# Low parts by VectorE instead of adding transfers, two fresh banks at the end and later gate rows in a diffusion transformer step

## The chip, the cores and the metric

One core of one Trainium2 chip runs the whole step. The metric is the device time of one execution in microseconds (us). TensorE (PE) multiplies; VectorE (DVE), ScalarE (ACT) and GpSimd (POOL) work on tiles; SyncE (SP) and POOL issue the transfers (DMA) that this text speaks of.

## The reference

One layer for 128 prompt tokens and 128 sample tokens, width 2048, all in float32. Both attention mixers use the result of one projection.

```python
sh1, sc1, g1, sh2, sc2, g2 = ada_mod(c, w_ada, b_ada)
h = rms_norm(x, norm1_w) * (1 + sc1) + sh1
qa, ka, va, qb, kb, vb, ga, gb = project_heads(h, w_in, ...)
oa = window_attention(qa, ka, va, ...)
ob = neighbourhood_attention(qb, kb, vb, ...)
x = x + g1 * ((sigmoid(ga) * (oa @ w_br_a) + sigmoid(gb) * (ob @ w_br_b)) @ w_out)
h2 = rms_norm(x, norm2_w) * (1 + sc2) + sh2
x = x + g2 * (square(relu(h2 @ w_up)) @ w_down)      # w_up 2048 x 8192, w_down 8192 x 2048
```

## The kernel before

Each weight tile of 128 x 1024 float32 numbers (512 KB) is a *step*; 456 steps, numbered 0 to 455, are multiplied in a fixed order. The matmuls take operands of the type fp32r (the profile names it), and every operand is split into a high part (`wH`, a copy by ScalarE at L108) and a low part (`wL`, the raw tile minus the high part, by VectorE at L268). A product is three matmuls: high by high, low by high, high by low. A plain step has twelve matmuls of 512 columns: three for each half of the tile and each of the two streams of tokens (prompt and sample).

The steps are: 0 to 72 the projection, 73 to 135 its gate columns, 136 to 199 the merge, 200 to 215 the first up columns. Then seven *pairs* follow, p = 1 to 7: sixteen steps of the up projection (`up_pair`, from step 216 + 32(p − 1)) and sixteen of the down projection (`down_unit`, four units of four steps). The last sixteen steps are the down projection of the last columns, where each unit ends in `resid`: VectorE multiplies the sum by the gate rows (`t<-g,acc`, L1138) and adds the residual (`x1b<-x1b,t`, L1142), and SyncE stores the result. The last unit (`last_unit`, steps 452 to 455) ends its second stream of tokens in two halves of 256 columns, so that the store of the first half can start.

In an up stage some of the eight positions are *fast* (list `FAST`): two weight tiles x and y give seven products in place of eight, of which the operands are made from the tiles. A fast position has these, with their lines: ScalarE's copies XH, YB (first half), tH, uH, and on VectorE t = x + y (L1465), XL (L1469), two sums in place (`raw`, L1470 and L1473), the low half of YB (L1472), tL (L1475) and uL (L1476). XL and YB's low half can also be made without VectorE: `minus_plus` lets ScalarE write minus the high part (L274), and a transfer issued by POOL then adds the weights from memory to it (L275). The lists `XL_DMA` and `YL_DMA` name the positions (8p + position) where this is done, and `LO_DMA` the plain steps. A value above zero is the number of steps by which the transfer goes ahead of its use; zero leaves it where the position is prepared.

The order on every engine is the order of the program, and that is made by `run()`: before the matmuls of a step it issues loads up to RUN further steps, then the adding transfers that are due, prepares the steps up to LOOK further (high and low parts), and copies high parts of AHEAD steps more. LOOK, RUN and AHEAD are strings with one digit for each step. Tiles come from a ring of 50 buffers of 512 KB; a load waits until its buffer has been read for the last time. The partial sums of the down projection (`dsum`) are put back as start values (*seeds*, `acc<-dsum`, by ScalarE) into the banks at the next pair's down units, and `DS_AWAY` names those that wait in memory meanwhile. `TE` names the heads whose probabilities TensorE transposes (L963); the others go through a transposing transfer. Gate columns of the projection that wait in memory (`AWAY`) come back GATE_BACK steps ahead, and the modulation of the layer is made beside the projection from `araw` tiles.

Of the kernel before, what the change touches and what calls it, by code (L numbers as in the profile page):

```python
# [18 lines left out]
P = 128  # L19
# [16 lines left out]
H_AT = 42  # L36
DOTS1 = [19, 26, 29, 33, 34, 34, 40, 42]
# [11 lines left out]
ADA_LD = [1, 0, 0, 2, 1, 0, 0]  # L49
BEGIN_SEED = ()  # L50
FAST = {1: (0, 1, 3, 7), 2: (0, 2, 4, 7), 3: (0, 3, 4, 5, 7), 4: (0, 2, 4, 6, 7), 5: (0, 1, 3, 6, 7), 6: (0, 1, 3, 6, 7), 7: (0, 2, 3, 5, 7)}
AWAY = [('gB', 2), ('gB', 0), ('gA', 0)]
GATE_BACK = 7
SEED_IN = {3: 0, 4: 1}
SEED_AT = 4
DIRECT = (3,)
LO_DMA = {123: 3, 162: 4, 196: 6, 205: 8, 233: 5, 421: 5, 452: 5}

LOOK = "220102342600004321112333333423344346003343323264425550024766435445100474621316521154444204744421242145443452135211233544444376555544342442445533113321545566643343457745545676631233475557402456897561133345442776554653214434322546645533234767635734543210333332754523544642203425555547355455542235444454346622143243143533120323340312252123324443413423323622444434555345666437402100223322544523544524557200014130212545432212544243022242111444300005772000137786"
RUN = "143538999224623021111226444342023133100001316655554435733333554564563325525103544635357136486300020025420321354421003432333255533612243352667454523663311454555543535997565577799967554203545745166866764795556988745674676472100044367288985999944454243112133555665422126411011224421346635244575533444454353423332446683456501300223410454545542322431521552123100123853233511252576696622311441202144625734434231022445134778334434464132124568676567978669999987788"  # L60
AHEAD = "822111111111101110000000111111110000000000122222221000000000000011122211000020133110000100000233100000000000002200000000000001112000000000000111000000100000000000000000011100000011111232221244332110000000000000000000000003011311110000000002000000000001020000000000000000000000000000002220001100100000000000000000000000000100000000000000001000222222222322320000000000000000000010000000000100000000000000000000000000000211110000000100000000012444242132345400"
CONST_AT = [63, 75]
XL_DMA = {9: 0, 11: 11, 16: 0, 20: 8, 23: 6, 26: 0, 29: 0, 36: 0, 37: 0, 38: 0, 43: 0, 46: 5, 53: 0, 54: 0, 63: 0}
ADA_G = ((1,), (2,), (3, 4), (5, 6))
ADA_AT = [None, 5, 14, 20, 22, 37, 38]
XS_AT = {1: 9, 2: 24, 3: 37}
POST = {('kvA', 0): [66, 70, 73], ('qA', 0): [65, 71, 75, 75, 77], ('qA', 1): [70, 74, 75, 76, 82], ('kB', 0): [74, 77, 79, 83, 85], ('qB', 0): [81, 82, 86, 88, 90], ('kB', 1): [84, 88, 91, 92, 97], ('qB', 1): [89, 92, 99, 100, 101]}
JOBS = [[79, 80, 82, 83, 85, 86, 89], [81, 83, 84, 86, 87, 92, 99], [86, 86, 87, 89, 91, 91, 106], [91, 92, 93, 96, 99, 105, 111], [93, 97, 99, 101, 101, 104, 115], [96, 101, 102, 104, 106, 106, 115], [106, 106, 108, 110, 117, 118, 125], [109, 111, 116, 117, 119, 123, 125]]
SS_G = [(0, 2), (2, 1)]
SS_AT = [50, 53, 71, 73, 131, 141]  # L70
T_AT = [3, 4]
PREP_IN = [6, 8]
DOTS = [33, 43, 47, 49, 50, 51, 52, 54, 56, 56, 56, 56, 60, 62, 63, 67, 70, 73, 80, 84, 89, 91, 92, 93, 96, 98, 102, 103, 104, 106, 108, 109, 109, 112, 114, 117, 118, 120, 122, 122, 126, 126, 129, 129, 129, 131, 132, 137, 138, 138, 140, 144, 145, 146, 154, 155, 156, 160, 160, 163, 167, 169, 173, 173, 175, 175, 179, 179, 180, 182, 184, 190]
DOTS2 = [222, 233, 234, 234, 235, 238, 245, 247, 254, 265, 269, 270, 272, 288, 300, 301, 304, 327, 328, 331, 333, 336, 349, 359, 360, 362, 364, 368, 393, 393, 395, 401]
STAT_AT = [4, -1, 9, 3]
T_PAIR = [[12, 6], [6, 10], [5, 10], [6, 10], [6, 10], [6, 10], [7, 12]]
P_PAIR = [[3, -1], [2, 4], [3, 3], [1, 4], [2, 5], [1, 5], [2, 0]]
M_TE = (3,)
M_AT = [2, 2, 5]
FLIP = 1  # L80
P_UP = [3, 3]
T_UP = [16, 11]
# [4 lines left out]
def tile_hybrid_step(ctx: ExitStack, tc: tile.TileContext, a):  # L87
# [143 lines left out]
    def add_step(src, mm, key, half=0, xkey=None):  # L231
# [10 lines left out]
        lead = LO_DMA.get(st["i"], 0) or XL_DMA.get(xkey, 0)  # L242
        load_at(st["i"] - LOAD - max(0, lead - LOAD), load)
# [64 lines left out]
    by_dma, xl_steps = [], []  # L308

    def run():  # L310
        loads.sort(key=lambda x: x[:2])
# [1496 lines left out]
```

## Time and profile before

| | us |
|---|---|
| median of 3 runs (1321.24 to 1321.27) | 1321.27 |
| the profiled execution | 1321.1 |
| span of its trace | 1319.3 |
| TensorE busy | 1306.7 |
| VectorE busy | 1123.5 |
| ScalarE busy | 905.1 |
| POOL busy | 57.1 |

Matmuls are pipelined: each 512-column matmul is recorded as about 0.39 us long but the next begins 0.23 us after it. So a gap on TensorE is read from the starts. A bracket behind a row names how long the engine was idle before it and what ended that.

### The profile page before, as it was taken

What the parts mean: (1) busy time and instruction counts of PE and PEld (TensorE: products, weight loads), DVE (VectorE), ACT (ScalarE), POOL (GpSimd) and SP (SyncE); (2) the same over time, 40 slices, a digit from 0 to 9 for tenths busy, and PEclk for the clock granted to TensorE, in tenths of its full rate; (3) what the DMA queues carried; (4) which work ended last, traced back from release to release, by engine and by line L of the source; (5) the groups of instructions that cost most, each with busy time, mean ns of one, the idle gap of its engine ahead of it and who ended that gap; (6) DMA issues with size and microseconds to landing.
All of it is one profiled execution on the core that took longest, in us unless ns stands there. A gap on an engine that the chain in (4) does not pass through costs nothing. (4 is left out here: it accounts for less than half of the span.)

```text
span 1319.3 us, 18022 instructions
## 1 busy us (share of the span) xinstructions
PE 1306.7 (99%) x6334; PEld 1057.9 (80%) x6335; DVE 1123.5 (85%) x1437; ACT 905.1 (69%) x1143; POOL 57.1 (4%) x65
## 2 busy tenths in 40 slices
PE   9999999999999999999999999999999999999998
PEld 4778778788888878888888888888888778878887
DVE  4669799988999999999788897997999899879474
ACT  5635655789866556536786868869778597787780
POOL 0000000431000000001000000000000000000000
PEclk9999999999999999999999999999999999999999
DMA  9999999998899989988798998778896886788861
GB/s 374 408 408 371 409 409 354 395 289 262 281 339 314 407 308 330 374 332 254 235 259 308 290 324 256 275 263 252 279 321 222 272 279 240 254 274 299 303 263 48
DMA packets 168939, 400.12 MB, mean 303 GB/s; under 512 B 70768, under 2 KB 72016, under 8 KB 168848
## 3 DMA queue, kind: packets, MB, share of 16 engines
q1 hardware_dynamic: 164688, 387.09, 81.3%
q0 software_dynamic: 4016, 11.80, 4.8%
q8 instruction: 49, 0.80, 0.2%
q14 instruction: 42, 0.34, 0.1%
q10 hardware_dynamic: 144, 0.08, 0.0%
HBM read 373.45 MB, written 10.80 MB: 291 GB/s over the span
## 5 line engine op out<-in xcount | busy, mean ns | idle before, releaser
L268 DVE TENSOR_TENSOR wL<-raw,wH 128x1024 fp32r<-128x1024 f32 x382 | 450.8, 1221 | 79.1 <-ACT wH L108 71.3
L108 ACT ACTIVATE wH<-raw 128x1024 fp32r<-128x1024 f32 (+1 forms) x396 | 393.2, 1040 | 107.5 <-DMA raw<-in_w_in 20.9
L467 PE MATMUL acc<-wH,hH 128*128 128x512 f32 x272 | 107.5, 395 | 0.6 <-ACT wH L108 0.6
L468 PE MATMUL acc<-wL,hH 128*128 128x512 f32 x272 | 105.9, 390 | 0.0
L469 PE MATMUL acc<-wH,hL 128*128 128x512 f32 x272 | 105.9, 389 | 0.0
L340 PE MATMUL acc<-wH,hH 128*128 128x512 f32 x252 | 100.7, 399 | 0.0
L342 PE MATMUL acc<-wH,hL 128*128 128x512 f32 x252 | 98.2, 390 | 0.0
L341 PE MATMUL acc<-wL,hH 128*128 128x512 f32 x252 | 98.2, 390 | 0.0
L1638 DVE CUSTOM_DVE_ANT_0 aT<-aT,cB,cols 128x1024 f32<-128x1024 f32 x56 | 71.5, 1283 | 0.6
L1638 DVE CUSTOM_DVE_ANT_0 junk<-aT,cB,cols 128x1024 bf16<-128x1024 f32 x56 | 71.5, 1284 | 0.0
L108 ACT ACTIVATE uH<-raw 128x1024 fp32r<-128x1024 f32 x33 | 35.1, 1063 | 45.0 <-DVE raw L1473 35.4
L467 PEld LDWEIGHTS acc<-wH,hH 128*128 128x128 f32 x272 | 51.1, 188 | 15.2 <-issue 2.9
L469 PEld LDWEIGHTS acc<-wH,hL 128*128 128x128 f32 x272 | 51.1, 188 | 10.8
L468 PEld LDWEIGHTS acc<-wL,hH 128*128 128x128 f32 x272 | 51.1, 188 | 10.1
L340 PEld LDWEIGHTS acc<-wH,hH 128*128 128x128 f32 x252 | 47.4, 188 | 10.4 <-issue 0.9
L341 PEld LDWEIGHTS acc<-wL,hH 128*128 128x128 f32 x252 | 47.4, 188 | 10.0 <-issue 0.5
L342 PEld LDWEIGHTS acc<-wH,hL 128*128 128x128 f32 x252 | 47.3, 188 | 9.9
L108 ACT ACTIVATE tH<-t 128x1024 fp32r<-128x1024 f32 x33 | 35.0, 1060 | 26.6 <-DVE t L1465 26.4
L1465 DVE TENSOR_TENSOR t<-raw 128x1024 f32<-128x1024 f32 x33 | 40.2, 1219 | 3.4 <-PE acc L342 2.3
L108 ACT ACTIVATE fTa<-pTa 128x2048 uint16<-128x2048 uint16 x16 | 40.6, 2535 | 1.5 <-DMA pTa<-pla 1.5
L1521 ACT ACTIVATE up<-up 128x1024 f32<-128x1024 f32 x28 | 29.7, 1062 | 17.1 <-DVE up L1511 16.7
L1476 DVE TENSOR_TENSOR uL<-raw,uH 128x1024 fp32r<-128x1024 f32 x33 | 40.4, 1225 | 0.9
(684 smaller groups left out, 3335.4 us busy)
## 6 DMA issues: line engine op xcount, KB each, us to landing
raw<-in_w_in SPq DMA_DIRECT2D x131, 512.0 KB, 9.0
raw<-in_w_down SPq DMA_DIRECT2D x128, 512.0 KB, 7.2
araw<-in_w_pair SPq DMA_DIRECT2D x80, 512.0 KB, 10.2
raw<-in_w_upF SPq DMA_DIRECT2D x66, 512.0 KB, 5.7
aT<-in_w_gT SPq DMA_DIRECT2D x64, 512.0 KB, 8.4
raw<-in_w_up SPq DMA_DIRECT2D x62, 512.0 KB, 6.0
aT<-in_w_adaT SPq DMA_DIRECT2D x48, 512.0 KB, 8.6
raw<-in_w_out SPq DMA_DIRECT2D x32, 512.0 KB, 8.9
```

The lines of the kernel that those rows point to most:

```text
L108: act.activation(out, in_, AF.Copy)
L268: dve.tensor_tensor(st["lo"], st["raw"], st["hi"].bitcast(F32), op=OP.subtract)
L340: pe.matmul(acc[tb], sh, wh[:, k, :], start=f, stop=False, **kw)
L341: pe.matmul(acc[tb], sh, wl[:, k, :], start=False, stop=False, **kw)
L342: pe.matmul(acc[tb], sl, wh[:, k, :], start=False, stop=l, **kw)
L467: pe.matmul(acc[tb], sh, wh[:, k, :], start=kt == 0 and k == 0 and not held and not seeded, stop=False, **kw)
L468: pe.matmul(acc[tb], sh, wl[:, k, :], start=False, stop=False, **kw)
L469: pe.matmul(acc[tb], sl, wh[:, k, :], start=False, stop=last and k == 1 and not hold, **kw)
L1465: dve.tensor_tensor(t.rearrange("p (a n) -> p a n", a=2), X.rearrange("p (a n) -> p a n", a=2), Y[:, 0:512].unsqueeze(1).to_broadcast([P, ...
L1476: dve.tensor_tensor(b["uL"], Y, b["uH"].bitcast(F32), op=OP.subtract)
L1521: act.activation(u.rearrange("p s n -> p (s n)"), u.rearrange("p s n -> p (s n)"), f)
L1638: dve.tensor_tensor_reduce(out, box["raw"], cB[s, tag], 1.0, dst if second else baT[:, part, fb:fb + 1], OP.mult, OP.add, dst)
```

## The change

- `XL_DMA` shrinks from twelve positions that are used to one, position 3 of pair 5 (43), which now goes 9 steps ahead and went where the position was prepared (5 steps ahead of its use). `YL_DMA` shrinks from ten to three. The title's "4 left of 22" are these. All other fast positions run as groups of seven VectorE instructions. `LO_DMA` has other plain steps: seven of its transfers are issued, of which three were before.
- The last unit multiplies the first stream of its last two steps in 512 columns, as before, and the second stream of both as 24 matmuls of 256 columns into two new banks. What the second stream had summed up to then is added to the residual earlier, by one more pair of VectorE instructions of 512 columns (`add_s`).
- The gate rows `g2` and the residual rows of the last four units are loaded 9 steps before the end of their own unit; before it was 6 steps before the end of the unit of the same columns in the preceding sixteen steps.
- `TE` loses one head group: its probabilities go through a transposing transfer (four transposes of TensorE and one copy less; two copies and one transfer more). `DS_AWAY` has four partial sums in memory in place of seven. The gate columns come back 9 steps later in the program (`GATE_BACK` 7 to −2; after the loads that are ahead, they are emitted at steps 136, 139 and 154 instead of 129, 133 and 147).
- `FAST` has other positions, as many in each pair. The tables of numbers for look-ahead, loads, dots and modulation have other values at many steps. `T_DMA` is empty and `G2_PARTS` is 1, so that the new functions for these are not used.

```diff
-TE = (('A', 0, 0), ('A', 0, 1), ('qA', 1), ('qB', 1))
-DS_AWAY = [0, 1, 2, 9, 13, 20, 22]
+TE = (('A', 0, 0), ('qA', 1), ('qB', 1))
+DS_AWAY = [9, 20, 22, 23]
-YL_DMA = [11, 15, 16, 23, 27, 31, 38, 39, 48, 56]
-PREP_LATE = 9
+YL_DMA = [9, 16, 31]
+T_DMA = {}
+G2_PARTS = 1
+PREP_LATE = 4
+G2_LEAD = 9
...
-GATE_BACK = 7
+GATE_BACK = -2
-LO_DMA = {123: 3, 162: 4, 196: 6, 205: 8, 233: 5, 421: 5, 452: 5}
+LO_DMA = {190: 14, 205: 8, 215: 9, 355: 5, 402: 6, 424: 7, 454: 6, 455: 3}
-XL_DMA = {9: 0, 11: 11, 16: 0, 20: 8, 23: 6, 26: 0, 29: 0, 36: 0, 37: 0, 38: 0, 43: 0, 46: 5, 53: 0, 54: 0, 63: 0}
+XL_DMA = {43: 9}
...
                 mms(q, 0)
                 if q < n - 2:
-                    mms(q, 1)
+                    mms(q, 1, end=n - 3)
+                if q == n - 3:
+                    add_s(box["acc"], 1)
                 if q == n - 1:
                     evac_s(box["acc"], 0)
-                    mms(q - 1, 1)
-                    for c in (slice(0, 256), slice(256, 512)):
-                        mms(q, 1, c)
-                        evac_s(box["acc"], 1, c)
+                    box["acc"] = [None, bank("acc"), bank("acc")]
+                    for i, c in enumerate((slice(0, 256), slice(256, 512))):
+                        for qq in (q - 1, q):
+                            mms(qq, 1, c, 1 + i, q - 1)
+                        evac_s(box["acc"][i:], 1, c)
...
-        e = end_of(("down", last - 1, n))
-        assert i + 6 < e
-        load_at(e - 6, lambda n=n: gate_bc("g2", n))
-        load_at(e - 6, lambda n=n: x1_back(n))
+        e = end_of(("down", last, n)) - G2_LEAD
+        assert g2_ready[n * G2_PARTS // 4] + 3 < e
+        load_at(e, lambda n=n: gate_bc("g2", n))
+        load_at(e, lambda n=n: x1_back(n))
```

How it moves instructions is shown at three places. The changed file has other line numbers: L111 is the copy that was L108, L277 the minus copy that was L274, L1358 to L1360 the matmuls that were L1351 to L1353, and L1505 to L1516 the group that was L1465 to L1476.

First TensorE at the end of the last unit, from the last 512-column matmul on; `a15H` and `a15L` are the stationary parts, and a bracket names the engine that a row waits for. Before:

```order
L1353 MATMUL acc<-wH,a15L 128x512
L1351 MATMUL acc<-wH,a15H 128x256
L1352 MATMUL acc<-wL,a15H 128x256
L1353 MATMUL acc<-wH,a15L 128x256
L1351 MATMUL acc<-wH,a15H 128x256
L1352 MATMUL acc<-wL,a15H 128x256
L1353 MATMUL acc<-wH,a15L 128x256
L1351 MATMUL acc<-wH,a15H 128x256 [waits DVE_49]
```

Now:

```order
L1360 MATMUL acc<-wH,a15L 128x512
L1358 MATMUL acc<-wH,a15H 128x256
L1359 MATMUL acc<-wL,a15H 128x256
L1360 MATMUL acc<-wH,a15L 128x256
L1358 MATMUL acc<-wH,a15H 128x256
L1359 MATMUL acc<-wL,a15H 128x256
L1360 MATMUL acc<-wH,a15L 128x256
L1358 MATMUL acc<-wH,a15H 128x256
```

The wait for VectorE between the halves is gone, and the last 512-column matmul shown is now the end of the first stream; twenty-four short ones follow it instead of twelve.

Second ScalarE ahead of pair 5, where the XL of its position 3 is copied; `dsum` rows belong to the down units of pair 4. Before, with the position's XH and XL in the middle:

```order
L108 ACTIVATE dsum_9246<-acc 128x512 x2
L108 ACTIVATE YB<-raw 128x512
L108 ACTIVATE tH<-t_9255 128x1024
L108 ACTIVATE uH<-raw 128x1024
L108 ACTIVATE wH<-raw 128x1024
L108 ACTIVATE XH<-raw 128x1024
L274 ACTIVATE XL<-XH 128x1024
```

Now:

```order
L111 ACTIVATE dsum_9138<-acc 128x512 x2
L111 ACTIVATE XH<-raw 128x1024 x2
L277 ACTIVATE XL<-XH 128x1024
L111 ACTIVATE YB<-raw 128x512
L111 ACTIVATE tH<-t_9184 128x1024
L111 ACTIVATE uH<-raw 128x1024
```

The copy, and with it the transfer by POOL, moved from behind the copies of the pair's earlier fast positions to ahead of them.

Third VectorE at position 0 of pair 7, where YB's low half came by a transfer. Before:

```order
L1465 TENSOR_TENSOR t_10647<-raw 128x1024
L1469 TENSOR_TENSOR XL<-raw,XH 128x1024
L1470 TENSOR_TENSOR raw<-t_10647,raw 128x512
L1473 TENSOR_TENSOR raw<-raw 128x512
L1475 TENSOR_TENSOR tL<-t_10647,tH 128x1024
L1476 TENSOR_TENSOR uL<-raw,uH 128x1024
```

Now:

```order
L1505 TENSOR_TENSOR t_10618<-raw 128x1024
L1509 TENSOR_TENSOR XL<-raw,XH 128x1024
L1510 TENSOR_TENSOR raw<-t_10618,raw 128x512
L1512 TENSOR_TENSOR YB<-raw,YB 128x512
L1513 TENSOR_TENSOR raw<-raw 128x512
L1515 TENSOR_TENSOR tL<-t_10618,tH 128x1024
L1516 TENSOR_TENSOR uL<-raw,uH 128x1024
```

The YB row came in ahead of the second sum, so that what follows on VectorE stands one instruction later.

More of the change, by code (lines that the diff above doesn't have):

```diff
@@ L69 @@
 SS_G = [(0, 2), (2, 1)]
[L70 to L74, printed above, removed]
@@ L1348, in mms @@
                 sh, sl = stat(q // 2)(2 * (q % 2) + k, tb)
-                kw = {"skip_group_check": True} if seed_from else {}
-                acc = box["acc"][tb][:, c]
-                pe.matmul(acc, sh, wh[:, k, c], start=q == 0 and k == 0 and not seed_from, stop=False, **kw)
+                seeded = seed_from and not begin_
+                kw = {"skip_group_check": True} if seeded else {}
+                acc = box["acc"][tb if to is None else to][:, c]
+                pe.matmul(acc, sh, wh[:, k, c], start=q == begin_ and k == 0 and not seeded, stop=False, **kw)
                 pe.matmul(acc, sh, wl[:, k, c], start=False, stop=False, **kw)
-                pe.matmul(acc, sl, wh[:, k, c], start=False, stop=q == n - 1 and k == 1, **kw)
+                pe.matmul(acc, sl, wh[:, k, c], start=False, stop=q == end and k == 1, **kw)
         for j, k0 in enumerate(ktiles):
@@ L1529, in up_pair @@
                     xl_steps.append((wsteps[-1]["i"] - XL_DMA[8 * p + pos], wsteps[-1]["i"]))
+                if nm == "y" and T_DMA.get(8 * p + pos):
+                    t_steps.append((wsteps[-2]["i"] - T_DMA[8 * p + pos], wsteps[-2]["i"], lambda b=b, f=sums_early: "raw" in b["x"] and f() or "load" in b["x"] and f()))
     dsum, dmem = {}, {}
@@ L1597, in tile_hybrid_step @@
     extra = {}
-    gcol = {n: cp.tile([P, 2, KC], F32, name=f"gc_{n}") for n in ("g1", "g2")}
+    gcol = {("g1", 0): cp.tile([P, 2, KC], F32, name="gc_g1")}
+    for g in range(G2_PARTS):
+        gcol["g2", g * KC // G2_PARTS] = cp.tile([P, 2, KC // G2_PARTS], F32, name=f"gc_g2{g}")
     cB = {}
@@ L1631, in dot @@
         which, fb = job
-        if which in gcol:
-            dst, part = gcol[which][:, s, fb:fb + 1], 2 + 3 * (which == "g2")
+        if which in ("g1", "g2"):
+            k0 = max(k for w, k in gcol if w == which and k <= fb)
+            dst, part = gcol[which, k0][:, s, fb - k0:fb - k0 + 1], 2 + 3 * (which == "g2")
         else:
```

125 lines of the change are left out of this document (84 added, 41 removed).

## The prediction

> **What bounds the kernel now.** I read the page first, then TensorE's waits, then the timeline around every wait of half a microsecond or more, then the work per pair of stages.
>
> ```profile
> PE 1306.7 (99%) x6334; PEld 1057.9 (80%) x6335; DVE 1123.5 (85%) x1437; ACT 905.1 (69%) x1143; POOL 57.1 (4%) x65
> ...
> PE Q L1409 <- DMA XL<-in_w_upF: 0.9, 1, 0.9
> PE Q L1409 <- DMA YB<-in_w_upF: 0.9, 1, 0.9
> ```
>
> TensorE is the bound: 99% busy, its clock granted in full. Time can be won only where TensorE stands still or by giving it fewer matmuls; everything else is a question of whether another engine comes late. The waits of TensorE (total us, times, longest) that the change speaks of are two: XL and YB are adding transfers, which it takes out. A wait's figure is less than its loss, since the pipeline also restarts; so I take the loss as the distance between two starts, less the usual step from one 512-column matmul to the next, 0.227 us (1031.38 to 1031.61 below is such a step).
>
> ```profile
> 1029.73 0.39 PE L1408 MATMUL Q<-XH,h21H 128*128 128x512 f32 x1
> 1031.05 0.50 PE L1409 MATMUL Q<-XL,h21H 128*128 128x512 f32 x1 [0.93 <-DMA XL<-in_w_upF]
> 1031.38 0.39 PE L1410 MATMUL Q<-XH,h21L 128*128 128x512 f32 x1
> 1031.61 0.40 PE L1408 MATMUL Q<-XH,sH 128*128 128x512 f32 x1
> ...
> DMA to landing us min/median/max: 5.2/6.0/10.9
> ...
> 1186.25 0.39 PE L1408 MATMUL Q<-YB,h20H 128*128 128x512 f32 x1
> 1187.52 0.50 PE L1409 MATMUL Q<-YB,h20H 128*128 128x512 f32 x1 [0.89 <-DMA YB<-in_w_upF]
> ```
>
> XL costs 1031.05 − 1029.73 − 0.23 = 1.09 and 0.10 in the next step: 1.2 us. YB costs 1.04 and the same restart, 1.15 us. The line between them gives XL's twelve transfers, issue to landing.
>
> **Tail.** The last unit's second stream, in one bank:
>
> ```profile
> 1311.19 0.39 PE L1351 MATMUL acc<-wH,a15H 128*128 128x512 f32 x1
> 1311.39 0.69 DVE L1138 TENSOR_TENSOR t<-g,acc 128x512 f32<-128x512 f32 x1 [5.13 <-PE acc L1353]
> ...
> 1312.55 0.28 PE L1351 MATMUL acc<-wH,a15H 128*128 128x256 f32 x1
> ...
> 1312.67 0.19 PEld L1353 LDWEIGHTS acc<-wH,a15L 128*128 128x128 f32 x1
> ...
> 1313.14 0.28 PE L1353 MATMUL acc<-wH,a15L 128*128 128x256 f32 x1
> 1313.46 0.42 DVE L1138 TENSOR_TENSOR t<-g,acc 128x256 f32<-128x256 f32 x1 [0.66 <-PE acc L1353]
> 1313.93 0.39 PE L1351 MATMUL acc<-wH,a15H 128*128 128x256 f32 x1 [0.52 <-DVE t L1138]
> ...
> 1314.63 0.28 PE L1353 MATMUL acc<-wH,a15L 128*128 128x256 f32 x1
> ```
>
> Six 512-column and twelve 256-column matmuls, with a hole after the sixth of the twelve: VectorE reads the bank that TensorE must write next. From the first start to the last it is 1314.63 − 1311.19 = 3.44 us. Afterwards there are 24 of 256 columns and no hole. Six of them stand 1312.55 to 1313.14, five steps of 0.118 us, so 23 steps take 2.71 us: the last matmul starts 0.73 us earlier, and what follows it (one t, one x1b, the store) is unchanged. New VectorE work here: t and x1b of the second stream up to the third step from the end, 2 × 0.69 = 1.4 us, which falls beside the twelve 512-column matmuls of the first stream (2.7 us) where VectorE idled 5.13 us before its t. The first half's t and x1b, 0.85 us, lie beside the second half's twelve (1.4 us). **Term: −0.73.**
>
> Only a rule says otherwise. The Trainium skill ("TensorE: Matmul & The Clock Gate", Part 3, The mechanism) has a weight load overlap running matmuls only when it goes to another row group. All loads here fill all 128 rows, and the rows above do not agree: a load is 0.19 us long and the matmuls are 0.118 apart, so they overlap. By the rule the change's six added loads would cost 1.1 us and the tail would lose 0.4 instead of winning 0.73. I go by the rows and keep the mechanism as a rival.
>
> **Adding transfers to VectorE.**
>
> ```profile
> L268 DVE TENSOR_TENSOR wL<-raw,wH 128x1024 fp32r<-128x1024 f32 x382 | 450.8, 1221 | 79.1 <-ACT wH L108 71.3 <-issue 2.7 <-ACT up L108 2.4
> L1469 DVE TENSOR_TENSOR XL<-raw,XH 128x1024 fp32r<-128x1024 f32 x21 | 25.6, 1218 | 0.0
> L1472 DVE TENSOR_TENSOR YB<-raw,YB 128x512 fp32r<-128x512 f32 x23 | 15.8, 685 | 0.4 <-ACT YB L108 0.4
> ...
> 678.80:1226.90 548.10, 544.71 (x2400) 449.78 (x2400) 482.31 (x541) 422.98 (x472) 17.89 (x21) 1.00 0.83 278
> 763.20:847.50 84.30, 84.30 (x374) 69.82 (x373) 76.36 (x89) 65.21 (x74) 2.56 (x3) 1.00 0.82 276
> 931.10:1014.80 83.70, 83.70 (x371) 69.31 (x370) 76.45 (x85) 68.37 (x78) 3.41 (x4) 1.00 0.80 261
> ```
>
> The last three rows give length, then busy PE, PEld, DVE, ACT: all the pairs, then pair 2 and pair 4, each with the down stage behind it. VectorE gets eleven XL of 1.218 and seven YB of 0.685, 18.2 us; two plain low parts fewer on balance (one comes back from a transfer, three go to one) give back 2.4 inside the pairs: +15.8 us. It has 548.1 − 482.3 = 65.8 us free there, and needs no TensorE time. By pair: 2 gets three XL and one YB, 4.3 us, and has 7.9 free; 4 gets two of each, 3.8 us, and has 7.25 free. So no pair makes VectorE the bound on average, and I cost this at nothing; the cover is some 3.5 us per pair in these two. Locally it is thinner. A fast position in seven VectorE instructions takes 4 × 1.22 + 3 × 0.69 = 6.9 us beside 21 matmuls of 0.227, 4.8 us. A plain one takes 2.4 beside 5.4. So VectorE falls 2.2 us behind at a fast position and wins 3.0 at a plain one; run-ahead must carry it. The thinnest row that I found is in pair 4's down stage:
>
> ```profile
> 977.71 1.22 DVE L268 TENSOR_TENSOR wL<-raw,wH 128x1024 fp32r<-128x1024 f32 x1 [0.47 <-ACT wH L108]
> ...
> 979.63 0.39 PE L341 MATMUL acc<-wL,a7H 128*128 128x512 f32 x1
> ```
>
> The low part is done at 978.93 and used at 979.63: 0.7 us of slack, in the pair that gets 3.8 us more, with the look-ahead of its steps nearly as it was. I take 0 to 1.5 us of new waits over the whole kernel, 0.3 as the value, since VectorE still waits 71.3 us for ScalarE's high parts, which is free time close to where work is added.
>
> What goes: the YB of the last pair's first position becomes a VectorE instruction like the 23 others, none of which TensorE waited for: **−1.15**. The XL of pair 5's position 3 stays a transfer but its copy and issue go from 5 steps ahead to 9. Four steps more are about 10 us; the missing time was 1.2: **−1.2**. The other transfers left or new are issued 5 steps or more ahead, at least 13 us, against at most 10.9 above: 0. The Trainium skill ("DMA: Bandwidth & Descriptors", Anatomy of one DMA) prices such a transfer at 2.0 us plus bytes over 436 GB/s, 3.2 us by an estimate for 512 KB; by it five steps were always enough, XL's −1.2 would not exist, and none left could come late. The measured 5.2 to 10.9 says that they queue, so I keep both.
>
> **One head's probabilities by DMA transpose** instead of TensorE:
>
> ```profile
> 298.04 0.60 PE L963 MATMUL ps_PT<-ident,prob 128*128 128x128 f32 x4
> 298.47 1.06 PE L913 MATMUL ps_S<-T_kvA,T_qA 128*128 128x128 f32 x8
> ```
>
> Four transposes go, 298.47 − 298.04 = 0.43 us: **−0.43**. The copies on ScalarE and the transpose that come in have 5 to 6 us to wait for, beside projection steps; 0.
>
> **Loads moved.** The last gate rows and residual rows now come 9 steps before their unit's end, 24 us; nothing asks for them sooner: 0. The gate loads of the merge come later (emitted at step 136 instead of 129):
>
> ```profile
> 452.20 2.67 SPq L349 DMA_DIRECT2D araw<-in_w_pair  x4
> ...
> 455.70 1.05 ACT L1011 ACTIVATE g_gA<-g_gA 128x1024 f32<-128x1024 f32 x1
> ...
> 462.19 2.01 ACT L108 ACTIVATE wH<-raw 128x1024 fp32r<-128x1024 f32 x2 [3.20 <-PE acc L341]
> g_gA<-gm_gA SPq DMA_DIRECT2D x1, 512.0 KB, 5.7
> ```
>
> SyncE issued the loads beside which the new place is at 452.20, and the transfer takes 5.7, so the sigmoid at 455.70 would wait till about 458, and high parts behind it some 2 us; the 3.20 us of ScalarE idle after them take it up: 0, at most +1. Three fewer round trips of partial sums hold three more of 50 buffers in pairs 0 to 3, where TensorE has no idle (84.30 of 84.30 above): 0. The early modulation loads are reordered; one stall among them:
>
> ```profile
> 153.37 0.64 PE L358 MATMUL ps_ada<-araw,cpad 128*32 128x256 f32 x8 [0.48 <-DMA araw<-in_w_pair]
> ```
>
> It may go (about −0.6) and others may come; I take 0, ends −0.7 and +0.7.
>
> **What stays.** The largest hole of the pairs:
>
> ```profile
> 1055.21 1.06 ACT L108 ACTIVATE wH<-raw 128x1024 fp32r<-128x1024 f32 x1 [2.60 <-DMA raw<-in_w_down]
> 1056.79 0.60 ACT L108 ACTIVATE acc<-dsum 128x512 f32<-128x512 f32 x1
> ...
> 1055.89 0.39 PE L1410 MATMUL Q<-XH,sL 128*128 128x512 f32 x1
> 1057.44 0.50 PE L340 MATMUL acc<-wH,a8H 128*128 128x512 f32 x1 [1.16 <-ACT acc L108]
> 1058.81 0.50 PE L340 MATMUL acc<-wH,a8H 128*128 128x512 f32 x1 [0.41 <-ACT acc L108]
> ```
>
> ScalarE stands 2.60 us for a weight load, and the seeds of the next accumulation queue behind it. TensorE loses 1.32, 0.58 and two restarts, about 2.1 us. The change keeps this order on ScalarE, and the buffer into which that weight goes is still freed by the same matmul of pair 5. So 0; −2.1 if its load starts earlier.
>
> **Sum:** −0.73 − 1.15 − 1.2 − 0.43 + 0.3 = −3.2 us. The profiled execution took 1321.1 us (1.8 outside its span) and the median is 1321.27, so 1318.1 in the median's terms.
>
> **Rivals.**
> *Better:* fewer transfers share the queues (eleven of 25 remain), pair 5's weight load lands 2.6 us earlier and the 1057 hole closes too, perhaps with the one at 153: 1318.1 − 2.1 − 0.6 = 1315.4. For it: the order is full of small margins. Against: the release of the buffer has not moved.
> *VectorE late in pairs 2 and 4:* in pair 4 the 3.8 us meet 0.7 of slack, 3.1; in pair 2, if its slack is the same, 4.3 leave 3.6. The full price is 6.7, which needs all spare time there to be useless; at half of it 1318.1 + 3.3 = 1321.4. For: the 0.7. Against: no wait for a low part by VectorE stands among TensorE's waits now.
> *Slower:* the same in every pair, because VectorE's free time lies where it waits for ScalarE and can't be used: of the 15.8 us more than 5.8, 37%, must reach TensorE to end above 1323.9; with half, 1318.1 + 7.9 = 1326.0. Against: the added instructions need only inputs that are there already.
> *Weight loads pace the short matmuls:* 24 × 0.19 instead of 24 × 0.118, +1.7: 1319.8. Against: the six at 0.118.
> *The change doesn't do what it says:* a transfer that is left lands late again (XL 1.2, or the last step's low part): 1319.3.
>
> **How the numbers follow.** 0.2% is 2.6 us, about what a measurement of this kernel tells from none: faster is below 1318.6, slower above 1323.9. Forecast (1317.0 to 1319.2) 0.46, about three quarters of it below 1318.6; better 0.19; late in two pairs 0.22; weight loads 0.03; a transfer late 0.04; slower 0.06. Faster 0.34 + 0.19 = 0.53, with a little of the late case 0.55; slower 0.07; same 0.38. The range leaves out the slower case and the ends of the two beside the forecast: 1315.2 to 1321.8.
>
> **What would show it.** Right: no XL or YB among TensorE's waits; the last unit's 24 matmuls 0.118 apart without the wait for t; VectorE about 1138 us busy; 4 transposes of L963's kind. The 1057 hole still there, some 1.6 us of seeds. Wrong: TensorE waiting for wL, XL or uL by VectorE in pairs 2 to 4, ScalarE waiting for DMA g_gA with TensorE idle after 458, or new araw waits in the first 200 us.

## The result, and the profile after

| | before | after |
|---|---|---|
| median, us | 1321.26 (1320.5 to 1321.27, 4 runs) | 1314.32 (1313.72 to 1314.89, 4 runs) |
| profiled execution, us | 1321.1 | 1313.9 |
| span of its trace, us | 1319.3 | 1312.1 |

The ratio is 0.9948, interval 0.9936 to 0.9960: 6.9 us faster, where 3.2 were forecast, and 0.9 below the range. The page of after, its first row and the rows of its transfer queues, and then all of TensorE's waits (total us, times, longest):

```profile
PE 1304.9 (99%) x6337; PEld 1058.2 (81%) x6337; DVE 1134.8 (86%) x1453; ACT 892.3 (68%) x1131; POOL 44.3 (3%) x51
...
q0 software_dynamic: 2000, 6.29, 2.4%
q8 instruction: 49, 0.80, 0.2%
```

```profile
PE ps_warm L135 <- DVE wm L128: 1.2, 1, 1.2
PE acc L473 <- ACT srow L111: 0.6, 1, 0.6
PE ps_sel L382 <- ACT S L111: 0.5, 1, 0.5
PE ps_ada L364 <- DMA araw<-in_w_pair: 0.3, 1, 0.3
PE ps_ss L170 <- ACT sq L167: 0.3, 1, 0.3
```

The adding transfers' queue, q0, has 6.29 MB where it had 11.80, and VectorE makes 11.3 us more. XL, YB, the seeds (`acc<-dsum`) and the last unit's t have left the list, and nothing made by VectorE in the pairs has come into it. The timelines of after at the three places, TensorE at XL, ScalarE and then TensorE ahead of pair 5's down stage, and TensorE and VectorE in the last unit:

```profile
1028.37 0.39 PE L1418 MATMUL Q<-XH,h21H 128*128 128x512 f32 x1
1028.59 0.39 PE L1419 MATMUL Q<-XL,h21H 128*128 128x512 f32 x1
...
1048.74 2.01 ACT L111 ACTIVATE wH<-raw 128x1024 fp32r<-128x1024 f32 x2 [2.65 <-PE Q L1419]
...
1051.26 0.60 ACT L111 ACTIVATE acc<-dsum 128x512 f32<-128x512 f32 x1
1052.82 0.60 ACT L111 ACTIVATE acc<-dsum 128x512 f32<-128x512 f32 x1 [0.96 <-DVE up L1551]
...
1053.30 0.39 PE L1420 MATMUL Q<-XH,sL 128*128 128x512 f32 x1
1053.53 0.39 PE L346 MATMUL acc<-wH,a8H 128*128 128x512 f32 x1
...
1305.03 0.39 PE L1360 MATMUL acc<-wH,a15L 128*128 128x512 f32 x1
1305.26 0.28 PE L1358 MATMUL acc<-wH,a15H 128*128 128x256 f32 x1
...
1308.01 0.28 PE L1360 MATMUL acc<-wH,a15L 128*128 128x256 f32 x1
...
1305.46 0.69 DVE L1144 TENSOR_TENSOR t<-g,acc 128x512 f32<-128x512 f32 x1 [1.31 <-PE acc L1360]
1306.18 0.69 DVE L1148 TENSOR_TENSOR x1b<-x1b,t 128x512 f32<-128x512 f32 x1
1306.89 0.42 DVE L1144 TENSOR_TENSOR t<-g,acc 128x256 f32<-128x256 f32 x1
1307.34 0.42 DVE L1148 TENSOR_TENSOR x1b<-x1b,t 128x256 f32<-128x256 f32 x1
```

XL follows the matmul ahead of it by 0.22, the usual step. The high part that ScalarE stood 2.60 us for at 1055.21 is now the second of the two copies in the row of 1048.74, which wait for TensorE and for no load; the seeds are done before they are wanted. The 24 short matmuls take 1308.01 − 1305.26 = 2.75, 0.12 apiece.

Where the 7.2 us of the two spans went is found by laying the k-th 512-column matmul of one trace beside the k-th of the other, so each stretch holds the same work:

| stretch | before to after, us |
|---|---|
| XL at 1031 | −1.22 |
| YB at 1187 | −1.17 |
| seeds of pair 5's down stage at 1057 | −2.16 |
| last unit, last 512-column matmul that both have to the last matmul (3.67 to 2.98) | −0.69 |
| `araw` at 153 | −0.69 |
| heads, around 298 | −0.14 |
| all other matmuls | −0.06 |
| the start, to the 100th matmul | −0.47 |
| last matmul to the end (4.70 to 4.11) | −0.59 |

The start is scatter between executions: the 100th of these matmuls begins at 49.64 to 50.37 us in the twelve traces of kernels built on before, and at 49.22 to 50.44 in the eight built on after. The end is not scatter alone: the last matmul begins 4.28 to 4.88 ahead of the end in the twelve (median 4.66) and 4.04 to 4.17 in the eight (median 4.12), whichever last unit a kernel has. The last store lands 3.07 to 3.14 us after that matmul begins in all twenty, so the difference lies in what the program does behind its last store; what makes it shorter in after is not known. So about 6 us have a place in the change, some 0.5 at the end go with it without a known cause, and 0.5 at the start is of this pair of executions.

### The profile page after: what moved, and what is told of

It reads as the page before. It is cut to its first block, busy times and chain, and to the rows that moved or that the text cites. A ratio compares the mean times of both kernels' runs of the same rounds, so it can differ in the third digit from the quotient of the medians.

```text
span 1312.1 us, 17946 instructions
## 1 busy us (share of the span) xinstructions
PE 1304.9 (99%) x6337; PEld 1058.2 (81%) x6337; DVE 1134.8 (86%) x1453; ACT 892.3 (68%) x1131; POOL 44.3 (3%) x51
## 3 DMA queue, kind: packets, MB, share of 16 engines
q0 software_dynamic: 2000, 6.29, 2.4%
## 4 chain that ended last, share of the span: by engine, by line
PE 97%; DMA 1%; ACT 1%; SPq 0%; issue 0%; DVE 0%; ACTq 0%
PE acc L346 17%; PE acc L348 17%; PE acc L347 17%; PE Q L1418 6%; PE Q L1420 6%; PE Q L1419 6%; PE acc L473 5%; PE acc L474 5%; PE acc L475 5%; PE ps_ada L364 3%; DMA araw<-in_w_pair 1%; PE ps_S L919 1%; PE Z L1418 1%; PE Z L1420 1%; PE Z L1419 1%; PE acc L1241 1%
## 5 line engine op out<-in xcount | busy, mean ns | idle before, releaser
L271 DVE TENSOR_TENSOR wL<-raw,wH 128x1024 fp32r<-128x1024 f32 x378 | 444.7, 1221 | 57.1 <-ACT wH L111 51.6
L111 ACT ACTIVATE wH<-raw 128x1024 fp32r<-128x1024 f32 (+1 forms) x396 | 391.8, 1039 | 94.2 <-DMA raw<-in_w_in 36.8
L111 ACT ACTIVATE uH<-raw 128x1024 fp32r<-128x1024 f32 x33 | 35.1, 1063 | 57.7 <-DVE raw L1513 55.7
L111 ACT ACTIVATE tH<-t 128x1024 fp32r<-128x1024 f32 x33 | 35.0, 1060 | 37.5 <-DVE t L1505 33.3
L1505 DVE TENSOR_TENSOR t<-raw 128x1024 f32<-128x1024 f32 x33 | 40.2, 1219 | 3.1 <-PE acc L348 2.3
L111 ACT ACTIVATE fTa<-pTa 128x2048 uint16<-128x2048 uint16 x16 | 40.6, 2536 | 1.4 <-DMA pTa<-pla 1.4
L1516 DVE TENSOR_TENSOR uL<-raw,uH 128x1024 fp32r<-128x1024 f32 x33 | 40.4, 1226 | 1.1
L1684 DVE CUSTOM_DVE_ANT_0 aT<-aT,cB,gc_g 128x1024 f32<-128x1024 f32 x32 | 40.6, 1281 | 0.4
```

The source lines that it names most:

```text
L111: act.activation(out, in_, AF.Copy)
L271: dve.tensor_tensor(st["lo"], st["raw"], st["hi"].bitcast(F32), op=OP.subtract)
L1684: dve.tensor_tensor_reduce(out, box["raw"], cB[s, tag], 1.0, dst if second else baT[:, part, fb:fb + 1], OP.mult, OP.add, dst)
```

## The experiments

The first six ask of the tail and of the transfers, the next ten of the hole at 1057 and of the whole sum, the last two of smaller terms. A time stands beside the median of the kernel before on the same chip, which was 1320.69 to 1321.27 in the five sets.

### The last unit

**The new last unit put into before** (`last_unit` and `add_s` of the change, all else as it was):

```diff
-                    mms(q - 1, 1)
-                    for c in (slice(0, 256), slice(256, 512)):
-                        mms(q, 1, c)
-                        evac_s(box["acc"], 1, c)
+                    box["acc"] = [None, bank("acc"), bank("acc")]
...
+                        for qq in (q - 1, q):
+                            mms(qq, 1, c, 1 + i, q - 1)
```

> The kernel before with the changed last unit alone (24 matmuls of 256 columns in two fresh banks, the earlier sum of the second stream). Theory A (the tail is worth what its matmuls are worth): the last matmul 0.73 us earlier against the last 512-column matmul, 1320.5. Rival B (the whole 1.28 us that the changed kernel won behind its last 512-column matmul belongs to the last unit): 1320.0. Nothing else moves: the waits for XL, YB and the seeds stay at 1.2, 1.15 and 2.1 us.

1320.66 beside 1321.0, ratio 0.9996 (0.9987 to 1.0005): the time can't resolve 0.7 us. The trace can:

```profile
1311.80 0.39 PE L1354 MATMUL acc<-wH,a15L 128*128 128x512 f32 x1
1312.02 0.28 PE L1352 MATMUL acc<-wH,a15H 128*128 128x256 f32 x1
...
1314.77 0.28 PE L1354 MATMUL acc<-wH,a15L 128*128 128x256 f32 x1
```

23 steps in 2.75 us, 0.12 each, no hole. The same stretch is 2.98 against 3.67, −0.69, and from the last matmul to the end it is 4.67, as long as before.

**After with the old last unit** (the same diff, taken back):

> The changed kernel with the old last unit. Theory A: its matmuls from the last 512-column one of the first stream on take 0.7 us longer, 1315.0. Rival B (the whole 1.28 us seen behind that matmul): 1315.6.

1314.8 beside 1321.27, ratio 0.9953 (0.994 to 0.9967), 0.5 above after, with overlapping intervals. In its trace the hole is back:

```profile
1307.99 0.28 PE L1359 MATMUL acc<-wH,a15L 128*128 128x256 f32 x1
1308.78 0.39 PE L1357 MATMUL acc<-wH,a15H 128*128 128x256 f32 x1 [0.51 <-DVE t L1144]
```

The stretch is 3.67 again. Both ways the last unit is worth 0.69.

### Transfers to VectorE

**Before with the two lists of after:**

```diff
-YL_DMA = [11, 15, 16, 23, 27, 31, 38, 39, 48, 56]
-XL_DMA = {9: 0, 11: 11, 16: 0, 20: 8, 23: 6, 26: 0, 29: 0, ...}
+YL_DMA = [9, 16, 31]
+XL_DMA = {43: 9}
```

> The kernel before with the changed lists of adding transfers for fast positions (XL of position 43 nine steps ahead, YB of 9, 16, 31; all else by VectorE), every other table as before. Theory T1 (the hole before pair 5's down stage closes because low parts by VectorE free buffers earlier): XL -1.2, YB -1.15 and the hole -2.1, 1316.8, and the weight of the fourth down step lands within 5 us. T2 (the hole was closed by the look-ahead tables) and T3 (by the partial sum that no longer comes back in pair 5): the hole stays, 1318.9. By the rival of a late VectorE in pairs 2 and 4: up to 3 us of new waits for wL, 1320 to 1322.

1317.19 beside 1321.0, ratio 0.9970 (0.9959 to 0.9981). XL and YB cost nothing, no wait for VectorE came into the pairs, and the hole at 1057 shrank from 2.16 to 0.57, of which the prediction had nothing. One new wait of 0.35 came at 613 us. That is more than half of the whole gain from two lines.

**Only the two late transfers** (XL of 43 earlier, YB of 56 to VectorE; the other transfers stay):

```diff
-YL_DMA = [11, 15, 16, 23, 27, 31, 38, 39, 48, 56]
+YL_DMA = [11, 15, 16, 23, 27, 31, 38, 39, 48]
-XL_DMA = {..., 43: 0, ...}
+XL_DMA = {..., 43: 9, ...}
```

> The kernel before with two transfers changed: XL of position 43 goes nine steps ahead, YB of position 56 by VectorE; the other twenty stay. By the sum of the prediction -2.35, 1318.9, with the hole of the seeds still 2.1 us. If the one late XL makes the hole (the same queue): 1316.8.

1318.24, ratio 0.9983 (0.9974 to 0.9993). In the profiled execution (1319.4) both waits went and the hole stayed at 1.75, but at the last fast position of pair 7 a transfer that had been just in time was now late:

```profile
1220.51 0.50 PE L1409 MATMUL Q<-XL,h22H 128*128 128x512 f32 x1 [0.65 <-DMA XL<-in_w_upF]
```

In before it landed 0.26 us ahead of its matmul; here it cost 0.98. So what the two edits win is worth 2.4 only if the next transfer has room, and taking nearly all of them out gave it. That the other executions lost as much there is not shown: the median fell by 2.8.

**After with the old lists:**

> The changed kernel with the lists of adding transfers of the kernel before (23 of them now fall on fast positions). Theory (what the change won in the pairs is the waits for late transfers): XL of pair 5 and YB of pair 7 wait again, 1 us each, and the hole before pair 5's down stage opens by 0.5 us or more: 1316.5 to 1318. Rival (the tables of look-ahead were made so that transfers land in time as well): 1314.3 to 1315.

1319.87 beside 1320.94, ratio 0.9993 (0.9982 to 1.0003): 5.5 above after. TensorE's waits have the reason:

```profile
PE Q L1419 <- DMA XL<-in_w_upF: 3.4, 3, 1.3
```

Three XL are late, at 860, 1034 and 1223 us, at a price of 1.32, 1.62 and 1.39. Of the two that were late in before, one is among them (pair 5's position 3, which goes late again) and YB is not. The hole at 1057 stays closed here, so it does not hang on the number of adding transfers alone.

**After with every XL of VectorE made twice**, the same result written again at 32 positions (39 us of VectorE):

```diff
                     dve.tensor_tensor(b["XL"], X, b["XH"].bitcast(F32), op=OP.subtract)
+                    dve.tensor_tensor(b["XL"], X, b["XH"].bitcast(F32), op=OP.subtract)
```

> The changed kernel with XL made twice by VectorE at each of the 32 fast positions where it is made by VectorE: 39 us more of VectorE work in the pairs, of some 50 us that are free there by the prediction's account. Theory (VectorE's free time can be used, run-ahead covers it): up to 3 us of new waits, 1314.5 to 1317.5. Rival (VectorE is at its limit after the change; more of its work reaches TensorE): a third or more of the 39 us, 1327 or above.

1341.28 beside 1321.27, ratio 1.0153 (1.0139 to 1.0167), so 27 of the 39 us reach TensorE:

```profile
PE acc L346 <- ACT acc L111: 4.7, 3, 2.1
PE Q L1419 <- DVE uL L1517: 3.3, 5, 0.8
PE Q L1418 <- ACT uH L111: 3.2, 3, 1.1
```

Through the pairs of after VectorE is idle for 50.7 of 543.5 us:

```profile
677.40:1220.90 543.50, 543.50 (x2399) 449.97 (x2399) 492.78 (x552) 411.34 (x460) 5.12 (x6) 1.00 0.75 258
```

Most of it can't be filled this way: the second XL stands ahead of the sums that ScalarE's uH waits for, and those waits of ScalarE rise from 55.7 to 92.7 us, so that TensorE waits for ScalarE too. The change's own 11 us found room; of 39 more, 12 did. Whether work at another place would fit better was not tried.

### The hole ahead of pair 5's down stage

This was 2.16 us that the prediction left standing. To compare kernels I count from t0, the start that the first matmul of that stage (step 360) would have had without a wait: 1056.12 in before, 1053.53 in after. SyncE's loads there, start and length of the issue, of before and then of after:

```profile
1036.33 7.84 SPq L239 DMA_DIRECT2D raw<-in_w_down  x2
1044.27 0.37 SPq L1627 DMA_DIRECT2D aT<-in_w_gT  x1
1044.74 0.38 SPq L239 DMA_DIRECT2D raw<-in_w_down  x1
1046.56 0.33 SPq L1627 DMA_DIRECT2D aT<-in_w_gT  x1
1047.92 0.80 SPq L239 DMA_DIRECT2D raw<-in_w_down  x2
```

```profile
1037.59 0.33 SPq L242 DMA_DIRECT2D raw<-in_w_down  x1
1041.25 0.33 SPq L1672 DMA_DIRECT2D aT<-in_w_gT  x1
1041.67 0.38 SPq L242 DMA_DIRECT2D raw<-in_w_down  x1
1042.16 0.37 SPq L1672 DMA_DIRECT2D aT<-in_w_gT  x1
1045.33 0.80 SPq L242 DMA_DIRECT2D raw<-in_w_down  x2
```

The load that ScalarE waits for is the first of the two in the last row of each view: issued at t0 − 8.19 in every kernel of the table below, before and after alike, as the prediction said. What moved is its landing, from t0 − 0.99 to t0 − 3.93. In before the second load of the first row is issued only at t0 − 12.28 (its buffer comes free by a matmul) and heads a burst of four; in after that load goes at t0 − 15.93 (freed by VectorE's tL), and the burst is three. There is a second neighbour. The page's row q8 is the fetching of instructions, 49 packets of 16 KB, each about 1 us long in the trace's transfer records and here some 29 us apart, and one of them passes at this place. All in us from t0:

| kernel | fetch starts | load lands | hole |
|---|---|---|---|
| before | −3.55 | −0.99 | 2.16 |
| only the two late transfers | −4.24 | −1.39 | 1.75 |
| digits alone | −4.30 | −1.51 | 1.64 |
| modulation loads alone | −3.94 | −1.13 | 2.01 |
| DS_AWAY without 13 | −2.59 | −2.63 | 0.51 |
| the two lists | −2.33 | −2.57 | 0.57 |
| lists and digits | −2.35 | −2.61 | 0.54 |
| before, fetch shifted | −15.19 | −2.59 | 0.57 |
| after without 355 | −2.09 | −2.94 | 0.21 |
| after, fetch shifted | −6.46 | −3.32 | 0 |
| before with 355 | −3.10 | −3.75 | 0 |
| after with the old digits | −2.20 | −3.80 | 0 |
| after | −2.09 | −3.93 | 0 |

Each row is one execution, the profiled one. Three more kernels fit the table: before with the new last unit, which changes nothing here (fetch −4.24, landing −1.33, hole 1.81), after with the old lists (−1.90, −3.51, 0) and the three parts of the change below (−3.40, −3.84, 0). The hole is the landing plus 3.15, and nothing when that is negative, to within 0.03 in every row. Two things move the landing: whether the fetch goes ahead of the load's end (the first four rows, −1.0 to −1.5) or elsewhere (the next four, −2.6), and the burst that is one load shorter (the last three, −3.75 to −3.93). The experiments behind these rows:

**Before, one partial sum less in memory:**

```diff
-DS_AWAY = [0, 1, 2, 9, 13, 20, 22]
+DS_AWAY = [0, 1, 2, 9, 20, 22]
```

> The kernel before with one partial sum less in memory (that of pair 3's second down unit, which came back in pair 5 beside the XL). T3: the hole of the seeds closes and perhaps XL's wait: 1318.0 to 1319.1. T1 and T2: no change at these places, 1321.2 plus or minus 0.4, or slower if the buffer that it holds is missed.

1320.99 beside 1321.0, ratio 1.0003 (0.9993 to 1.0012). In its trace the hole is 0.51 with XL (1.18) and YB (1.33) still there. The burst is that of before, and ScalarE's wait is short:

```profile
1053.73 1.06 ACT L108 ACTIVATE wH<-raw 128x1024 fp32r<-128x1024 f32 x1 [0.95 <-DMA raw<-in_w_down]
```

In this execution most of the hole was closed without a change in the loads here, and that led to the fetch. It was the fastest of ten (1319.96), and the median did not move, so it is not shown that the edit closed the hole in the others.

**The fetch shifted, in before**, by 80 more tiny instructions of TensorE at the start (F in the expectations is the theory that the fetch's place sets the hole):

```diff
-    warm(9)
+    warm(4)
+    tick(45)          # 45 matmuls of 8 columns
```

> The kernel before; the nine warm-up matmuls at the start are four, and 45 of 8 columns follow them, so that 80 more instructions of TensorE lie ahead of everything. Theory F (the hole before pair 5's down stage is made by a 16 KB transfer of instructions, which in the kernel before begins 3.55 us ahead of the hole's step and holds up the weight load that lands 1.0 us ahead of it): such transfers come once in some 29 us of TensorE's program, this one comes about 9 us earlier, the load lands 2.5 us ahead of the step and the hole falls from 2.2 to about 0.5 us; about 1319.6. Rival (buffers and the order of loads alone make the hole): 2.2 us as before, 1321.2.

1321.74 beside 1320.94, ratio 1.001 (1.0 to 1.0019). The fetch went to −15.19, the load landed at −2.59 and the hole was 0.57. The time shows none of it, and the rest of the account can't be closed. The profiled execution was 4.7 us above its own median. It lost 4.7 from 680 us on, first 2.2 in a wait of TensorE for ScalarE's `up` at a granted clock of 1.00, then most of the rest while the clock was 0.66 (684 to 688 us) and 0.91 (688 to 692). And of the 1.6 won at the hole it lost 1.33 at pair 7, where the XL that was late with the two transfers changed was late here too.

**The fetch shifted, in after**, by 30 instructions:

```diff
-    warm(9)
+    warm(6)
+    tick(18)
```

> The changed kernel with 30 more instructions of TensorE ahead of everything (six warm-up matmuls and 18 of 8 columns for nine). There the transfer of instructions begins 2.1 us ahead of the same step, behind the weight load (landed 3.9 ahead). Theory F: it comes about 3 us earlier, ahead of that landing, which falls to some 2.5 us ahead, and 0.3 to 0.7 us of the hole come back. Rival (the change closed the hole by freeing buffers earlier, and has room): 0 as now, 1314.3.

1315.13, ratio 0.9951 (0.9934 to 0.9967). The fetch at −6.46 is ahead of the load, which lands 0.6 later than in after, and there is no hole: after has room for a fetch. F alone missed here.

**Dots moved off the stretch, in before:**

```diff
-DOTS2 = [..., 349, 359, 360, 362, 364, 368, 393, ...]
+DOTS2 = [..., 349, 367, 368, 369, 370, 371, 393, ...]
```

> The kernel before with five gate dot products of steps 359 to 368 moved to steps 367 to 371 (one table), so that two of their loads no longer stand ahead of the weight load on which the hole before pair 5's down stage hangs. Theory Q (that load waits for its turn behind four others): it lands 1.3 us or more sooner relative to the step, and the hole falls from 2.2 to 0.6 or less, whether or not the transfer of instructions falls ahead of it; 1319.4. Rival (the hole hangs on when the load's buffer comes free, which is where it was): 2 us as before. XL and YB wait as before, 1.2 each.

1322.73 beside 1321.27, ratio 1.0017 (1.0007 to 1.0027). With the dots' `aT` loads out of the burst the weight load goes at t0 − 11.37 in place of −8.19 and lands at −6.13, so the hole is 0. The kernel is slower all the same, since pair 6 pays 2.84 for it, by these rows among others:

```profile
1101.13 0.50 PE L1408 MATMUL Q<-XH,h20H 128*128 128x512 f32 x1 [0.67 <-ACT dsum L108]
1106.98 0.50 PE L1409 MATMUL Q<-XL,h20H 128*128 128x512 f32 x1 [0.56 <-DVE XL L1469]
1110.05 0.50 PE L1409 MATMUL Q<-tL,sH 128*128 128x512 f32 x1 [0.73 <-DVE tL L1475]
```

**The digits of the look-ahead, steps 328 to 375** (D: these digits shorten the burst), put into before alone, into before with the lists, and back to the old ones in after. Of the three strings, RUN:

```diff
-RUN[328:376] = "104545455423224315215521231001238532335112525766"
+RUN[328:376] = "124545444533124215215521231001338532335122535656"
```

> The kernel before with the changed digits of look-ahead, loads and high parts ahead for steps 328 to 375 alone. Theory D (these digits free a buffer for one load ahead of the burst, which in the changed kernel is issued 15.9 us ahead of the hole's step and was issued 12.3 ahead): the load on which the hole hangs lands about 1.3 us sooner than without the digits, the hole is 0 to 0.6 us in place of 2.2, about 1319.6. Rival (the digits leave it; the lists of transfers or the partial sums moved the buffer): loads at 12.3 us ahead as before and a hole of 0.5 or 2, by the transfer of instructions.

> The kernel before with the changed lists of adding transfers for fast positions and the changed digits of steps 328 to 375. Theory D: XL -1.3, YB -1.2 and the hole closed to 0, 1316.4 to 1317; rival: as the lists alone, 1317.2, with a hole of 0.5 to 2.

> The changed kernel with the old digits of steps 328 to 375. Theory D: the hole comes back, 0.5 us where the transfer of instructions falls behind the load and 2 where it falls ahead, 1315 to 1316.5. Rival: no hole, 1314.3.

The digits alone: 1321.04 beside 1320.69, ratio 1.0005 (0.9995 to 1.0015), hole 1.64, burst unchanged. With the lists: 1317.13, ratio 0.9973 (0.9964 to 0.9983), hole 0.54, as the lists alone. After with the old digits: 1314.46, ratio 0.9955 (0.994 to 0.997), no hole. D is false three times.

**One adding transfer more, in before** (L: the low part of step 355, in pair 5's up stage, comes by a transfer in after; its buffer is taken from the ring at another place, and so are the buffers behind it):

```diff
-LO_DMA = {123: 3, 162: 4, 196: 6, 205: 8, 233: 5, 421: 5, 452: 5}
+LO_DMA = {123: 3, 162: 4, 196: 6, 205: 8, 233: 5, 421: 5, 452: 5, 355: 5}
```

> The kernel before with one more adding transfer: the low part of plain step 355, five steps ahead, as the changed kernel has it. Theory L: its buffer is taken at another place of the ring, so that the second weight load for pair 5's down stage waits for VectorE and no longer for TensorE; it is issued some 16 us ahead of the hole's step in place of 12.3, one load less queues in front of the fourth, which lands 2.4 us or more ahead of the step, and the hole is 0 to 0.7 in place of 2: 1319.3 to 1319.8, XL and YB late as before. Rival: the hole stays as in the kernel before.

1319.72 beside 1321.18, ratio 0.9986 (0.9977 to 0.9996). The load that headed the burst now goes at −18.36, freed by tL as in after, the one that ScalarE waits for lands at −3.75, and ScalarE no longer stands for it:

```profile
1051.88 2.01 ACT L108 ACTIVATE wH<-raw 128x1024 fp32r<-128x1024 f32 x2 [3.97 <-PE Q L1410]
1054.41 0.60 ACT L108 ACTIVATE acc<-dsum 128x512 f32<-128x512 f32 x1
```

XL (1.35) and YB (1.05) stay. L is shown: an adding transfer *more* closes the hole, and the median falls by 1.5.

**After without it** (355 out of `LO_DMA`):

> The changed kernel without the transfer for step 355 (its low part by VectorE). Theory L: the load waits for TensorE again, 12.3 us ahead, and the hole comes back: 0.5 us where the transfer of instructions falls behind the fourth load's landing, 2 where it falls ahead: 1314.8 to 1316.3. Rival: no hole, 1314.3.

1314.81, ratio 0.9951 (0.9936 to 0.9966). The load is back at −12.27, freed by a matmul, and the hole is 0.21: L holds in direction, but here the fetch stands behind the load and leaves little to win.

**Three parts of the change together in before** (the two lists, 355, the new last unit; nothing else):

> The kernel before with three pieces of the change: the lists of adding transfers of fast positions, the transfer for step 355 and the last unit. Theory: XL -1.2, YB -1.2, the hole -2, the tail -0.7 against 1320.9: 1315.8, some 1.5 above the changed kernel, which also has the earlier araw loads (0.7 to 0.9) and the four transposes (0.4). Rival (the other tables were needed to keep VectorE in time): 1317 or more.

1315.76 beside 1321.18, ratio 0.9958 (0.9942 to 0.9975), 5.4 us of the 6.9. The holes at XL, YB, the seeds and the last unit are all closed. What is left to after is 1.4 us, with overlapping intervals; the traces offer the 0.69 at `araw` and the 0.14 at the heads, which stay here, and 0.19 at the end (4.30 against 4.11). The later gate rows, GATE_BACK and the other positions of `FAST` were not tried alone; the table of stretches leaves them next to nothing ahead of the last matmul.

### Two smaller terms

**The modulation's order in before:**

```diff
-ADA_LD = [1, 0, 0, 2, 1, 0, 0]
-ADA_AT = [None, 5, 14, 20, 22, 37, 38]
+ADA_LD = [-1, 1, 0, 0, 0, 0, 0]
+ADA_AT = [None, 5, 14, 18, 22, 37, 40]
```

> The kernel before with the changed places of the modulation loads and of their matmuls alone (two tables). Theory: the wait for araw at 153 us, 0.7, goes, and the start may win up to 0.5: 1320.1 to 1320.6. Rival (the tables of look-ahead and loads did it): the wait stays, 1321.2.

1321.59 beside 1320.94, ratio 1.0002 (0.9992 to 1.0011). The stall at 153 us is gone as in after (0.7), and 0.55 at 93 and 0.8 at 174 to 178 us came instead. So the order takes the stall away, and alone it wins nothing; what in after keeps the other two away was not found.

**After without any head transposed by TensorE for A's first group:**

```diff
-TE = (('A', 0, 0), ('qA', 1), ('qB', 1))
+TE = (('qA', 1), ('qB', 1))
```

> The changed kernel with the last head group's probabilities also by the transposing transfer (the four remaining transposes of TensorE of this kind go). By the price in the prediction: -0.43, 1313.9. Rival: the transfer comes late for its use, plus 1 to 3 us.

1313.67, ratio 0.9947 (0.9934 to 0.9961), as after within the interval. The trace shows no gain: there are four transposes fewer and a wait in their place, and that stretch is 0.44 longer than in after:

```profile
PE acc L347 <- DVE wL L271: 0.8, 1, 0.8
```

## Why the prediction was right and wrong

**Tail, −0.73: right**, 0.69 both ways round. The rival that weight loads pace the short matmuls (+1.7) is false: they stand 0.12 apart. The rule of the Trainium skill ("TensorE: Matmul & The Clock Gate", Part 3, The mechanism) that went with it does not show itself here; the same section also lets a load run ahead when it goes to the background weight buffer, and no run here tells which of the two applies.

**XL −1.2 and YB −1.15: right**, 1.22 and 1.17. The working that more steps ahead suffice was sound for the XL that is left, which went out 8.0 us before its matmul was due in before (1021.91 and 1029.96) and goes out 21.8 before it in after (1006.81 and 1028.59). The prediction's "at least 13 us" for five steps was too much, as those 8.0 show. And the rival of a transfer that lands late is real: with the old transfers kept, in before at pair 7 and in after at three places, others took their turn.

**VectorE +0.3: nothing.** No wait for VectorE came into the pairs, so the rivals of VectorE late are false for this change. The prediction's worry was of the right size, though. It put the point from which the slow case decides at 37% of the added work reaching TensorE, and of 39 us added 27, 69%, did. The change adds 11.3 over the whole kernel, and that fits.

**Four transposes, −0.43: less.** They are gone, but the stretch won 0.14; in the timeline of after one step there is 0.42 long, since its weight load stood 0.46 us for wL, and that takes most of the rest:

```profile
309.07 0.39 PE L346 MATMUL acc<-wH,hH 128*128 128x512 f32 x1
309.49 0.50 PE L347 MATMUL acc<-wL,hH 128*128 128x512 f32 x1
```

**Loads moved, 0 with −0.7 to be had at 153 us: the lower end**, −0.69. The sigmoid and the gate rows made no new wait.

**"What stays": wrong, and the largest miss.** It kept the 2.1 us at 1057 because "the buffer into which that weight goes is still freed by the same matmul". That is true, the load is issued at −8.19 in both. The step that failed is the next one, from the same issue to the same landing. The prediction let the hole close only if the load started earlier. The load lands 2.9 us earlier from the same start, because one load fewer is queued ahead of it (355) and because a fetch of instructions no longer goes ahead of it; each alone closes 1.6 to 2.16 of it in before. The first is the change's doing. The second is luck as far as is known: no line of the change aims at the fetch. Either would nearly do, for after without 355 has a hole of only 0.21. The rival *Better* had this number (1315.4) and a cause of the same kind, queues with less in them; but fewer adding transfers was not it, since one more of them closes the hole in before and 23 on after's kernel leave it closed.

With the hole at −2.16, `araw` at −0.69 and 0 for VectorE, the prediction's own sum would have been −0.73 − 1.15 − 1.2 − 0.14 − 2.16 − 0.69 = −6.1, or 1315.2; after's median is 0.9 below. The t, x1b and store behind the last matmul are unchanged, as it said; about 0.5 is won behind the store (the medians of 4.66 and 4.12), and for that it had no term. The rest is within the scatter of the start (−0.47 in the profiled pair). Whether that is all stays open.

## What to carry to other kernels

Judge a load that is waited for by its landing: count what is queued ahead of it when it is issued, for the same issue landed 2.9 us earlier with one load fewer and a fetch out of the way. Where a ring hands out buffers in the program's order, an edit that takes one buffer at another place moves all loads behind it, so look at the waits near every such place and not only at the edited one. When transfers are just in time, closing one wait can open the next (0.98 at pair 7, 2.84 at pair 6, 1.4 at the modulation); an edit that frees room for all of them, as the two lists did, keeps its gain.

## What the hardware showed that I had not expected

Fetching TensorE's own instructions counts among the transfers: 16 KB, about 1 us, yet in before's kernels a load that it went ahead of landed 1.1 to 1.6 us later (−1.0 to −1.5 against −2.6), and in after 0.6 later (−3.32 against −3.93). The moment of the fetch against the same step moves between executions of nearly the same program, from −4.3 to −2.1; 80 tiny instructions at the start moved it by 12 us. Why it costs more than its own length, and why it moves without a change of the instructions, stays open.

Idle time of VectorE at 86% busy was usable only in part: of 39 us added to it at one place of each fast position, 27 came out at the end.
